# Pool's convolution taps in accumulators of their own, and two TensorE steps moved, in a two-layer hybrid decoder trunk

## The chip, the cores and the metric

The kernel runs on one core of one Trainium2 chip. A core has five engines that run side by side, each with its own queue of instructions: TensorE (PE, matmuls; PEld is its weight load), VectorE (DVE), ScalarE (ACT), GpSimd (POOL) and SyncE (SP, which issues DMAs; POOL issues some too). An engine takes its instructions in the order in which they were written, so one that waits holds up all behind it. The metric is the device time of one execution in microseconds; smaller is better.

## The reference

Two layers (`DEPTH = 2`) of width 1024 over 256 positions. Each layer is a SwiGLU FFN, a token-mixing stage and a second FFN, each with adaLN modulation. The change lies in the mixing stage, which projects its normalised input once and works on three groups of columns:

```
h = a * sigmoid(gate)                                   # group A, 256 channels
h = depthwise_causal_conv(h, w)  # 31 taps; then LayerNorm over channels, SiLU

softmax attention, 6 heads of 64 with partial rotary    # group B

q, k, v = silu(short_conv(qkv))                         # group C, 6 heads of 64, chunked delta rule
g = cumsum(-exp(a_log) * softplus(a + dt_bias));  beta = sigmoid(b)
L = strict_lower(k_beta k^T * decay(g));  T = inverse(I + L)
u = T v_beta, ...;  o = rmsnorm(...) * silu(z)
```

The three outputs are concatenated and go through one output projection. All arithmetic is float32; matmuls split their operands into a high and a low part and use three products.

## The kernel before, in words

All weights (253 MB in the profile) are streamed through four raw buffers of 1 MB by SP's queue. ACT rounds each piece to a high part (`hi`), DVE subtracts for the low part (`lo`), and PE multiplies. The adaLN vectors are summed by DVE from their own weight pieces (`adaacc`, `Lb`).

The instruction order is fixed when the program is written, by a planner inside the kernel. `Clock` keeps a modelled time for each engine and for each tile the modelled time at which it is ready. The main stream of PE is the projection, unit by unit; after each step of it, `tick()` goes through a list of side generators (`sides`): key and query norms, decays, pairs, gate and convolution, values, inverse, delta rule, attention, taps. A generator that yields tiles, such as `yield (v,)`, goes on once these are ready by the modelled clock; `yield from until("v")` waits for an event of that name, and `room()` for a free PSUM bank. What a generator then emits stands in the engines' queues at that place, whatever the real times are.

The parts that the change touches:

- `decays()` computes the log decays' exponentials. `spread(b)` has DVE write 128x1024 spread rows into `Rs` (tiles `Lb` and `S6a`); a small product of `g[:, 0]` (tile `g_g`) with the constant `gt` gives `cross` (tile `g_c`), the bias of one of the three exponentials of each head. Before the change this product stands directly behind the emission of the first two spreads.
- `values_beta()` turns v (tile `v`) by six PE transposes into `vb`, as soon as `gate_conv()` has emitted v's SiLU (event `v`). `delta_rule()` is the first to use `vb`, after the event `inverse`.
- `inverse()` inverts I + L. The matrix LT (tile `xin_LT`, views `LD` and `LX`) is written to memory (`scr_l`, by `pairs()`) and read back as `Lb`, both by POOL's DMA queue; POOL then does a substitution of 15 steps on 16x16 blocks (tiles `T` and `W`), writes the result to `scr_w` and reads it back as `Wc`; PE, ACT and DVE join the blocks. While the substitution is planned, `cfg["lo_pool"]` is False, and taps go to DVE alone.
- `tap(b, fast)` does one of the 31 taps of channel block b (b = 0, 1) on the 128x256 accumulator `cacc["ca"][:, b]` (tile `cacc`). The first is a DVE `tensor_scalar`; a fast one is a DVE `scalar_tensor_tensor`; a slow one has ACT write the product into a tile `ctap` (two buffers) and POOL add it to the same accumulator. `taps(b)` takes the slow form where DVE is over 2 us ahead of PE by the modelled clock; `fill()` puts a tap where DVE would stand still.
- `convolution()` sums the accumulators over the channels, normalises and applies SiLU; the output projection of blocks 0 and 1 follows.

The tags `rstd` and `gr` name two small buffers (the norm's reciprocal roots, the gates' rows) whose contents have been used up when the taps begin.

Nearly all engine calls go through one helper, so nearly every row of the profile says L171, and instructions are told apart by their tiles (`pa`, `pm` and `px` are PSUM banks).

Of the kernel before, what the change touches and what calls it, by code (L numbers as in the profile page):

```python
# [10 lines left out]
F32 = mybir.dt.float32  # L11
# [3 lines left out]
OP = mybir.AluOpType  # L15
# [4 lines left out]
S = 256  # L20
# [5 lines left out]
NH = 6  # L26
# [151 lines left out]
def trunk(ctx, tc, t, out):  # L178
# [5 lines left out]
    act, dve, pe, gp, sp, qd = (clock.engine(n, e) for n, e in (  # L184
        ("act", nc.scalar), ("dve", nc.vector), ("pe", nc.tensor), ("gp", nc.gpsimd), ("dma", nc.sync), ("dma2", nc.gpsimd)))

    def sb(shape, tag, dt=F32, bufs=1):
        return clock.tile(tag, bufs, pool.tile(shape, dt, name=tag, tag=tag, bufs=bufs))
# [10 lines left out]
    def mm(o, lhsT, rhs, start, stop=True):  # L199
        pe.matmul(o, lhsT, rhs, start=start, stop=stop, skip_group_check=True)  # L200
# [55 lines left out]
    p = ps([128, 128], "x")  # L256
# [753 lines left out]
    def mixing(l, G, normed, nxt):  # L1010
# [4 lines left out]
        ev = {}  # L1015
# [21 lines left out]
        def room(n=1):  # L1037

            while True:
                times = sorted(freed(x) for x in side_tags() if x not in held.values())  # L1040
                if len(times) > n and times[n - 1] <= clock.t["pe"]:
                    return
                yield

        def pside(shape, hold=False):
            tag = min((x for x in side_tags() if x not in held.values()), key=freed)
            p = latest[tag] = ps(shape, tag)
            if hold:
                held[p.tensor.name] = tag
            return p  # L1050
# [7 lines left out]
        def until(*names):  # L1058
            while any(n not in ev for n in names):
                yield  # L1060
# [137 lines left out]
        def decays():  # L1198
            yield from until("g", "kconv")
            g, lnbeta = ev["g"], ev["lnbeta"]  # L1200
            while any(job[1].tensor.name.startswith("Lb") for job in ada_wait):
                extract()
            g, heads = g
            Rs = [sb([128, 1024], tag, F32R).rearrange("p (s k i x) -> p s k i x", s=2, k=2, i=2) for tag in ("Lb", "S6a")]
            cross = sb([128, NH], "g_c")

            def spread(b):
                dve.tensor_tensor(Rs[b % 2].rearrange("p s k i x -> p (s k i) x"), K["tri"][:, 0:128].unsqueeze(1).to_broadcast([128, 8, 128]),
                                  heads[:, 2 * b:2 * b + 2].rearrange("p h k i -> p (h k i)").unsqueeze(2).to_broadcast([128, 8, 128]),
                                  op=OP.mult)  # L1210

            spread(0)
            spread(1)
            yield from room()
            p = pside([128, NH])
            mm(p, gt.bitcast(F32), g[:, 0], True)
            dve.tensor_tensor(cross, p, lnbeta[:, 0, NH:], op=OP.add)
            for b in range(3):
                R = Rs[b % 2]
                yield (R,)  # L1220
                yield from room(2)
                d = pside([128, 2, 2, 128], True)
                x = pside([128, 2, 128], True)
                for k in range(2):
                    mm(d, gt, R[:, :, k], k == 0, False)
                mm(d, identb, negdb.unsqueeze(1).to_broadcast([128, 4, 128]), False, True)
                for k in range(2):
                    mm(x, onesr, R[:, :, k, 1], k == 0, k == 1)
                if b == 0:
                    spread(2)  # L1230
                yield from until("ktable")
                yield (x,)
                let_go(d)
                let_go(x)
                for s in range(2):
                    h = 2 * b + s
                    act.activation(PT[:, h, 0:128], d[:, s, 0], AF.Exp, bias=lnbeta[:, 0, NH + h:NH + h + 1])
                    act.activation(PT[:, h, 128:256], x[:, s], AF.Exp, bias=cross[:, h:h + 1])
                    act.activation(PT[:, h, 256:384], d[:, s, 1], AF.Exp, bias=lnbeta[:, 1, NH + h:NH + h + 1])
                    ev["decay", h] = True  # L1240
            yield from until("kh")
            act.preload_act_table_set("silu_and_others")
            ev["silu2"] = True
# [31 lines left out]
            ev["PT"] = True  # L1275

        def values_beta():
            yield from until("v")
            v = ev["v"]
            vb = sb([128, 2, 384], "vb")  # L1280
            for i in range(2):
                yield (v,)
                yield from room()
                p = pside([128, 384])
                for b in range(3):
                    pe.transpose(p[:, 128 * b:128 * b + 128], v[:, b, HALF[i]], ident)
                act.copy(vb[:, i], p)
            ev["vb"] = vb
# [81 lines left out]
        def inverse():  # L1370
# [21 lines left out]
                yield idle("gp")  # L1392
            gp.tensor_copy(W[:, 1], V.rearrange("p c i -> p i c"))
            cfg["lo_pool"] = True
            C = sb([128, 2, 12, 32], "Wc")
            for f in range(2):
                for i in range(2):
# [17 lines left out]
            p, o = joined()  # L1415
# [8 lines left out]
            p, o = joined()  # L1424
# [17 lines left out]
            p, o = joined()  # L1442
# [53 lines left out]
            ev["exp2"] = True  # L1496


        cacc, left = {}, {}

        def tap(b, fast=True):

            hc, ca, k = ev["glu"], cacc["ca"], left[b] - 1
            wof = CB["conv_w"]
            w = cB[:, wof + 2 * k + b:wof + 2 * k + b + 1]
            if k == CONVK - 1:
                dve.tensor_scalar(ca[:, b], hc[:, b, k:k + S], w, cA[:, CA["conv_b"] + b:CA["conv_b"] + b + 1],
                                  op0=OP.mult, op1=OP.add)
            elif fast:
                dve.scalar_tensor_tensor(ca[:, b], hc[:, b, k:k + S], w, ca[:, b], op0=OP.mult, op1=OP.add)  # L1510
            else:
                m = sb([128, S], "ctap", bufs=2)
                act.activation(m, hc[:, b, k:k + S], AF.Copy, scale=w)
                gp.tensor_tensor(ca[:, b], ca[:, b], m, op=OP.add)
            left[b] = k

        def fill():
# [7 lines left out]
        def taps(b):  # L1525
            yield from until("glu")
            if "ca" not in cacc:
                cacc["ca"] = sb([128, 2, S], "cacc")
            left[b] = CONVK
            clock.filler = fill  # L1530
            while left[b]:
                yield idle_any(("dve",), ("act", "gp")) if cfg["lo_pool"] else idle("dve")
                if left[b]:
                    tap(b, left[b] == CONVK or clock.t["dve"] <= clock.t["pe"] + AHEAD)
            ev["taps", b] = True

        def convolution():
            yield from until(("taps", 0), ("taps", 1), "exp2")
            ca = cacc["ca"]
            yield (ca,)  # L1540
            yield from room()
            p = pside([128, S], True)
            for b in range(2):
                mm(p, ones, ca[:, b], b == 0, b == 1)
            yield soon(p)
            let_go(p)
            dve.scalar_tensor_tensor(ca, p.unsqueeze(1).to_broadcast([128, 2, S]), -1.0 / 256, ca, op0=OP.mult, op1=OP.add)
            sq = tmp([128, 2, S])
            yield (ca,)
            act.activation(sq, ca, AF.Square)  # L1550
            yield (sq,)
            yield from room()
            p = pside([128, S], True)
            for b in range(2):
                mm(p, ones, sq[:, b], b == 0, b == 1)
            r = tmp([128, S])
            yield soon(p)
            let_go(p)
            act.activation(r, p, AF.Ln, bias=eps, scale=1.0 / 256)
            act.activation(r, r, AF.Exp, scale=-0.5)  # L1560
            yield (r,)
            dve.tensor_tensor(ca, ca, r.unsqueeze(1).to_broadcast([128, 2, S]), op=OP.mult)
            yield from until("softmaxed", "zraw", *["gdn_normed"] * ("u" in ev))
            act.preload_act_table_set("silu_and_others")
            act.activation(ev["zraw"], ev["zraw"], AF.Silu)
            ev["z"] = ev["zraw"]
            for b in range(2):
                act.activation(ca[:, b], ca[:, b], AF.Silu, scale=cA[:, CA["conv_ln_g"] + b:CA["conv_ln_g"] + b + 1],
                               bias=cA[:, CA["conv_ln_b"] + b:CA["conv_ln_b"] + b + 1])
            act.copy(yh[:, 0:2], ca)  # L1570
            dve.tensor_tensor(yl[:, 0:2], ca, yh[:, 0:2], op=OP.subtract)
            ev["conv_done"] = True
# [420 lines left out]
```

## Time and profile before

| | us |
|---|---|
| median of three runs | 1190.27 |
| lowest and highest | 1187.80, 1190.31 |
| the profiled execution, its own time | 1185.86 |
| span of the profiled execution, first to last instruction | 1184.1 |
| PE busy | 1118.8 (94%) |
| DVE busy | 880.2 (74%) |
| ACT busy | 596.9 (50%) |
| POOL busy | 142.0 (12%) |

The mean granted TensorE clock is 0.980 of full speed. A busy PE is not PE at its peak. In the span the first layer's mixing stage lies roughly between 250 and 400 us, the second's between 820 and 975; the rest is FFNs. A row of the timeline has the start, the duration, the engine, the operation and its tiles, the count, and in brackets the idle time of the engine just before it with what ended it. A row of the table of stretches gives each engine's busy time in that stretch, then the granted clock.

### The profile page before, as it was taken

How to read it: one execution, taken by the hardware profiler on the slowest of the kernel's cores; microseconds unless marked ns; L12 is line 12 of the kernel's file. 1: busy time of each engine (PE TensorE's matmuls, PEld its weight loads, DVE VectorE, ACT ScalarE, POOL GpSimd, SP SyncE). 2: the span in 40 equal slices, each digit the busy share in tenths (PEclk: the TensorE clock that was granted, in tenths of full speed). 3: DMA queues.
4: the chain of work that ended last, by engine and by line, in shares of the span. 5: the costliest groups of instructions: out<-in, count | busy, mean ns of one | idle time of the engine just before them, and what ended most of it. 6: DMA issues, size and time to landing. Idle time of an engine off the chain costs nothing. (4 is left out here: it accounts for less than half of the span.)

```text
span 1184.1 us, 21996 instructions
## 1 busy us (share of the span) xinstructions
PE 1118.8 (94%) x9085; PEld 1042.9 (88%) x9085; DVE 880.2 (74%) x1354; ACT 596.9 (50%) x1007; POOL 142.0 (12%) x185
## 2 busy tenths in 40 slices
PE   5799999999899689999999999999989998999997
PEld 4799999967778689999999999997768898999996
DVE  6778778757897788868779878773869959766554
ACT  4364444447366364544456544434743676544443
POOL 0710000010650010000001000001037101000002
PEclk9899999999999989999999999999998999999999
DMA  9759888836333558968864997793552325876740
GB/s 325 249 174 353 291 309 311 245 105 201 99 127 123 174 182 290 328 236 320 302 227 161 329 333 256 279 302 92 168 165 74 144 81 170 304 247 214 203 136 36
DMA packets 167660, 256.52 MB, mean 217 GB/s; under 512 B 8272, under 2 KB 134056, under 8 KB 167560
## 3 DMA queue, kind: packets, MB, share of 16 engines
q1 hardware_dynamic: 166536, 252.95, 63.1%
q0 software_dynamic: 1024, 2.16, 0.9%
q8 instruction: 71, 1.16, 0.4%
q14 instruction: 29, 0.24, 0.1%
HBM read 252.86 MB, written 2.23 MB: 215 GB/s over the span
## 5 line engine op out<-in xcount | busy, mean ns | idle before, releaser
L171 PE MATMUL pm<-H,hi 128*128 128x256 f32 x2816 | 509.2, 283 | 1.2 <-DVE H L171 1.2
L171 DVE TENSOR_TENSOR lo<-raw,hi 128x1024 fp32r<-128x1024 f32 (+1 forms) x300 | 362.6, 1230 | 101.2 <-ACT hi L171 100.3
L171 PEld LDWEIGHTS pm<-H,hi 128*128 128x128 f32 x2816 | 432.3, 189 | 5.1 <-issue 1.6
L171 ACT CAST hi<-raw 128x1024 fp32r<-128x1024 f32 (+1 forms) x306 | 311.4, 1041 | 190.7 <-PE pm L171 77.0
L171 PE MATMUL pm<-H,lo 128*128 128x256 f32 x1408 | 392.1, 280 | 0.0
L171 PEld LDWEIGHTS pm<-H,lo 128*128 128x128 f32 x1408 | 264.8, 189 | 0.0
L171 PE MATMUL pa<-Y,hi 128*128 128x256 f32 x1312 | 235.3, 283 | 3.5 <-DVE xT L171 2.7
L171 PEld LDWEIGHTS pa<-Y,hi 128*128 128x128 f32 x1312 | 201.6, 190 | 4.7 <-DVE xT L171 3.5
L171 PE MATMUL pa<-Y,lo 128*128 128x256 f32 x656 | 184.1, 281 | 0.0
L171 PEld LDWEIGHTS pa<-Y,lo 128*128 128x128 f32 x656 | 125.8, 192 | 0.0
L171 POOL TENSOR_TENSOR xin_LT<-xin_LT 128x256 f32<-128x256 f32 x35 | 27.2, 776 | 667.5 <-ACT xin_LT L171 665.1
L171 ACT CAST Y<-tmp 128x256 fp32r<-128x256 f32 x88 | 35.8, 406 | 121.2 <-DVE tmp L171 121.2
L171 DVE SCALAR_TENSOR_TENSOR adaacc<-raw,c_act,adaacc 128x1024 f32<-128x1024 f32 x70 | 94.2, 1346 | 1.6
L171 DVE SCALAR_TENSOR_TENSOR Lb<-raw,c_act,Lb 128x1024 f32<-128x1024 f32 x56 | 71.8, 1282 | 4.3 <-DMA raw<-in_w_ada_dram 3.0
L171 DVE TENSOR_TENSOR Y<-tmp,Y 128x256 fp32r<-128x256 f32 x88 | 37.4, 425 | 41.6 <-ACT Y L171 41.6
L171 PE MATMUL pm<-Y,raw 128*128 128x256 f32 x288 | 67.5, 384 | 0.0
L171 PEld LDWEIGHTS pm<-Y,raw 128*128 128x128 f32 x288 | 53.1, 190 | 7.9
L171 PE MATMUL pa<-hi,Y 128*128 128x512 f32 x176 | 54.8, 393 | 0.0
L171 DVE SCALAR_TENSOR_TENSOR cacc<-hc,colB,cacc 128x256 f32<-128x256 f32 x94 | 47.9, 528 | 8.0 <-POOL cacc L171 6.8
L171 ACT ACTIVATE tmp<-pm 128x256 f32<-128x256 f32 x78 | 29.6, 380 | 47.7 <-PE pm L171 47.7
L171 DVE TENSOR_REDUCE mod<-px 128x4 f32<-128x512 f32 x34 | 23.4, 690 | 38.4 <-PE px L171 38.4
L171 POOL TENSOR_TENSOR cacc<-cacc,ctap 128x256 f32<-128x256 f32 x26 | 26.0, 1010 | 131.0 <-ACT ctap L171 126.0
(303 smaller groups left out, 1311.2 us busy)
## 6 DMA issues: line engine op xcount, KB each, us to landing
raw<-in_w_ada_dram SPq DMA_DIRECT2D x70, 1024.0 KB
raw<-in_ffn_w_gate_dram SPq DMA_DIRECT2D x44, 1024.0 KB
raw<-in_ffn_w_up_dram SPq DMA_DIRECT2D x44, 1024.0 KB
raw<-in_ffn_w_down_dram SPq DMA_DIRECT2D x44, 1024.0 KB
raw<-in_w_in_dram SPq DMA_DIRECT2D x12, 1024.0 KB
raw<-in_w_in_dram SPq DMA_DIRECT2D x20, 512.0 KB
raw<-in_w_out_dram SPq DMA_DIRECT2D x16, 512.0 KB
raw<-in_w_in_dram SPq DMA_DIRECT2D x4, 768.0 KB
```

Source lines behind the costliest of these rows:

```text
L171: return getattr(real, op)(*args, **kw)
```

## The change

Three edits in `mixing()`.

1. Pool's taps get accumulators of their own, one for each channel block, in the buffers `rstd` and `gr`. The first slow tap of a block is written there by ACT without a POOL instruction; each later one is a product of ACT in `ctap` and an addition of POOL to that accumulator. `convolution()` begins with a DVE addition of each such accumulator to `ca`.
2. `values_beta()` also waits for a new event `back`, which `inverse()` sets when the substitution has been emitted.
3. In `decays()` the product for `cross` moves behind the wait for the first spread rows.

```
@@ decays @@
             spread(0)
             spread(1)
-            yield from room()
-            p = pside([128, NH])
-            mm(p, gt.bitcast(F32), g[:, 0], True)
-            dve.tensor_tensor(cross, p, lnbeta[:, 0, NH:], op=OP.add)
             for b in range(3):
                 R = Rs[b % 2]
                 yield (R,)
+                if b == 0:
+                    yield from room()
+                    p = pside([128, NH])
+                    mm(p, gt.bitcast(F32), g[:, 0], True)
+                    dve.tensor_tensor(cross, p, lnbeta[:, 0, NH:], op=OP.add)
                 yield from room(2)
@@ values_beta @@
-            yield from until("v")
+            yield from until("v", "back")
@@ inverse @@
             gp.tensor_copy(W[:, 1], V.rearrange("p c i -> p i c"))
             cfg["lo_pool"] = True
+            ev["back"] = True
@@ tap @@
-        cacc, left = {}, {}
+        cacc, left, shared = {}, {}, set()
...
+            other = cacc["gp"][b]
...
             else:
-                m = sb([128, S], "ctap", bufs=2)
+                m = sb([128, S], "ctap", bufs=2) if b in shared else other
                 act.activation(m, hc[:, b, k:k + S], AF.Copy, scale=w)
-                gp.tensor_tensor(ca[:, b], ca[:, b], m, op=OP.add)
+                if b in shared:
+                    gp.tensor_tensor(other, other, m, op=OP.add)
+                shared.add(b)
@@ taps @@
                 cacc["ca"] = sb([128, 2, S], "cacc")
+                cacc["gp"] = [sb([128, S], tag) for tag in ("rstd", "gr")]
@@ convolution @@
             ca = cacc["ca"]
+            for b in sorted(shared):
+                yield (cacc["gp"][b],)
+                dve.tensor_tensor(ca[:, b], ca[:, b], cacc["gp"][b], op=OP.add)
             yield (ca,)
```

## The prediction

> **What bounds the kernel now.** I read the page's busy shares first, then who PE (TensorE) waited for, over the whole run.
>
> ```profile
> span 1184.1 us, 21996 instructions
> ...
> PE 1118.8 (94%) x9085; PEld 1042.9 (88%) x9085; DVE 880.2 (74%) x1354; ACT 596.9 (50%) x1007; POOL 142.0 (12%) x185
> ```
>
> ```profile
> PE pa L171 <- ACT v L171: 9.2, 2, 4.7
> ...
> PE pa L171 <- DVE g_g L171: 3.2, 2, 1.6
> ```
>
> PE is the bound, so time is gained only where PE stands still or runs slowly. Columns of the waits: total, times, longest. Both lines occur twice, once in each layer's mixing stage, and the diff's second and third edits move exactly these two PE instructions. The timeline of the first layer shows how the longer wait comes about (start, duration, instruction; in brackets the engine's idle time before it, and its releaser).
>
> ```profile
> 290.58 0.61 DVE L171 TENSOR_TENSOR xin_LT<-pa,PT 128x256 f32<-128x256 f32 x2
> ...
> 295.85 0.73 POOL L171 TENSOR_TENSOR cacc<-cacc,ctap 128x256 f32<-128x256 f32 x1 [52.44 <-ACT ctap L171]
> 296.52 2.48 POOL L171 DMA_DIRECT2D scr_l<-xin_LT  x4
> 296.88 0.51 ACT L171 ACTIVATE ctap<-hc,colB 128x256 f32<-128x256 f32 x1
> ...
> 304.03 1.45 POOL L171 DMA_DIRECT2D Lb<-scr_l  x2 [5.03 <-DMA scr_l<-xin_LT]
> 305.50 0.75 POOL L171 TENSOR_TENSOR cacc<-cacc,ctap 128x256 f32<-128x256 f32 x1
> 306.28 0.88 DVE L171 SCALAR_TENSOR_TENSOR cacc<-hc,colB,cacc 128x256 f32<-128x256 f32 x2 [2.69 <-POOL cacc L171]
> 307.07 1.51 DVE L171 SCALAR_TENSOR_TENSOR v<-pm,colB,v 128x255 f32<-128x255 f32 x3
> 308.66 1.28 ACT L171 ACT_TABLE_LOAD   x1 [6.47 <-DVE v L171]
> ...
> 310.85 0.90 PE L171 MATMUL pa<-kc,v 128*128 128x128 f32 x3 [4.50 <-ACT v L171]
> ```
>
> The product of Pool's second tap was ready at 297.4 (296.88 plus 0.51), but its addition stands in POOL's queue behind the DMA that reads `scr_l` back, and that one waits for the write to land. DVE's next tap on the same accumulator therefore waits 2.69, v's convolution behind it on DVE is late, ACT's table load and SiLU of v are late, and PE stands at the transposes of v, with all matmuls behind them.
>
> A second thing stands there: the matrix LT (`xin_LT`) was complete at 291.2, yet POOL issued its DMA at 296.5, because the first tap's addition was ahead in the queue, waiting for ACT. The second layer repeats all of it:
>
> ```profile
> 864.69 0.61 DVE L171 TENSOR_TENSOR xin_LT<-pa,PT 128x256 f32<-128x256 f32 x2
> ...
> 870.63 2.45 POOL L171 DMA_DIRECT2D scr_l<-xin_LT  x4
> ...
> 880.56 0.88 DVE L171 SCALAR_TENSOR_TENSOR cacc<-hc,colB,cacc 128x256 f32<-128x256 f32 x2 [2.86 <-POOL cacc L171]
> ...
> 885.14 0.90 PE L171 MATMUL pa<-kc,v 128*128 128x128 f32 x3 [4.67 <-ACT v L171]
> ```
>
> After each of these waits the granted clock (the column behind POOL's) is low; this is the table of stretches:
>
> ```profile
> core 0: us, PE busy (x) PEld busy (x) DVE busy (x) ACT busy (x) POOL busy (x), PEclk, DMA share, GB/s
> 310.85:313.50 2.65, 2.65 (x7) 1.51 (x8) 1.07 (x4) 2.51 (x5) 2.18 (x7) 0.50 0.00 0
> 885.14:890.40 5.26, 5.26 (x19) 4.12 (x20) 3.66 (x8) 4.19 (x7) 4.40 (x12) 0.50 0.01 3
> 904.30:911.10 6.80, 6.80 (x28) 6.17 (x29) 6.66 (x16) 3.04 (x9) 6.52 (x8) 0.50 0.25 58
> ```
>
> **The change, part by part.**
>
> *Values behind the substitution.* The six transposes of v are emitted only after Pool's substitution has been planned, so later in PE's stream, when v is long done. They and ACT's two copies into `vb` stay as many as before. `vb` is first used by the delta rule, after the inverse, so nobody is behind them. PE loses the wait: 4.50 + 4.67 = 9.2. It also loses the half clock behind it: 2.65 and 5.26 us at 0.50 cost half, 1.3 + 2.6 = 3.9. What is late next on PE are the query products, which need the same SiLU and the table load behind it; the order is planned again, and they stay where the planned time of the queries puts them, so other matmuls fill the gap. That the third stretch (904.3 to 911.1, no wait before it) goes too, worth 3.4, I don't count; it is the fast end.
>
> [...]
>
> *Pool's own accumulators.* The first slow tap of each of the two channel blocks becomes one ACT instruction that writes the accumulator directly; its POOL addition goes. The other additions stay, on Pool's own tile. DVE's chain no longer waits for POOL: 2.69 and 2.86 less DVE waiting, so v's SiLU is that much earlier (in the gain above already, since PE no longer waits for v). Nothing of POOL is ahead of the `scr_l` DMA any more, so it can issue at 291.2 instead of 296.5: 5.3 earlier in each layer. Added: one DVE addition per block at the end, 128x256, two a layer, each below the 0.68 of DVE's 128x512 product in the next fence. Their cover:
>
> ```profile
> 377.18 0.68 DVE L171 TENSOR_TENSOR cacc<-cacc,tmp 128x512 f32<-128x512 f32 x1
> ...
> 386.28 1.28 ACT L171 ACT_TABLE_LOAD   x1
> ```
>
> The normalised convolution is done at 377.9 and used only after the table load that waits for PE's z, at 386.3: 8.4 us hide at most 1.4. If PE reaches z 7 us earlier than now and the taps don't follow, 1.4 is left, just enough. If the cover were gone it would cost up to 1.4 a layer.
>
> *Log decays' product behind the spread rows.* The product needs g, the end of a DVE chain of small operations; PE meets it too early:
>
> ```profile
> 259.65 0.17 DVE L171 TENSOR_TENSOR g_g<-g_x,g_ea 128x12 f32<-128x12 f32 x1
> ...
> 259.88 0.39 PE L171 MATMUL pa<-g_g,gt 128*128 128x6 f32 x2 [1.61 <-DVE g_g L171]
> ...
> 267.50 0.63 ACT L171 ACTIVATE tmp<-S3a 128x512 f32<-128x512 f32 x1
> ...
> 268.19 1.12 PE L171 MATMUL pa<-tmp,kc 128*128 128x512 f32 x2
> ```
>
> ```profile
> 834.00 0.39 PE L171 MATMUL pa<-g_g,gt 128*128 128x6 f32 x2 [1.62 <-DVE g_g L171]
> ```
>
> The waits are 1.61 and 1.62, together 3.2, and go. The bounds of what stays are 0 and 3.2: the key norm's product at 268.19 starts 0.06 after its squares are ready (267.50 plus 0.63), which DVE and ACT set, so PE can lose there what it gained, unless the new order puts more matmuls ahead. The order does count PE's wait for g in its plan, so some will move; between the ends I take half, 1.6. DVE's small addition behind the product comes later in DVE's queue, and ACT's exponentials need it; a delay there is within that half.
>
> *What takes the place.* The next thing that PE can meet is the first product of the inverse, which needs Pool's whole chain (LT to `scr_l`, back, substitution, `scr_w`, back as `Wc`):
>
> ```profile
> 330.06 2.09 POOL L171 DMA_DIRECT2D Wc<-scr_w  x2
> ...
> 334.38 1.01 PE L171 MATMUL pa<-Wc,Lb 32*32 32x32 f32 x96
> ```
>
> ```profile
> 903.87 2.09 POOL L171 DMA_DIRECT2D Wc<-scr_w  x2
> ...
> 912.77 1.02 PE L171 MATMUL pa<-Wc,Lb 32*32 32x32 f32 x96
> ```
>
> ```profile
> DMA to landing us min/median/max: 4.0/4.1/4.3
> ```
>
> ```profile
> 291.20:334.40 43.20, 38.66 (x233) 32.86 (x233) 33.36 (x72) 18.38 (x34) 29.20 (x53) 0.96 0.41 119
> 865.30:912.90 47.60, 42.93 (x245) 36.85 (x247) 37.91 (x79) 22.43 (x46) 31.96 (x55) 0.86 0.39 108
> ```
>
> `Wc` lands 4.1 after its issue, at 334.2 and 908.0: the chain takes 43.0 and 42.7 from LT. 5.3 earlier makes 37.7 and 37.4. PE's own work in the same stretches, at full clock, is 38.66 less 1.3 = 37.3 and 42.93 less 6.0 (half of 5.26 + 6.80) = 36.9. So new waits of 0.4 and 0.5 come out. The unknown is when `scr_l` lands: issued earlier, it runs beside other weight transfers. Bounds: 0 (the chain fully hidden) and 11.4 (nothing of the 5.3 gained: 5.7 + 5.8). I take 2.0, near the worked value.
>
> **The sum.** 9.2 + 3.9 + 3.2 gained is 16.3; 1.6 and 2.0 come back; 12.7 stay. The profiled execution took 1185.9 (span 1184.1), so 1173.2 for it. The median of the three runs shown is 1190.3, 4.4 above it; taken from the median the forecast is 1177.6. The tails of both layers and the FFNs behind hang on PE's progress and shift with it.
>
> **The rivals.**
>
> *A: Pool's chain becomes the wait.* `scr_l` lands no earlier, since the transfers beside it hold it up (POOL waited 5.03 for it even now). Then the first layer's stretch stays at 43.0 of 43.2 and the second's comes to 42.7 of 47.5: gains 0.2 and 4.8, plus 1.6 from the log decays: 6.6, time 1183.7. For it: the window is just as full of weights. Against it: the write starts 5.3 earlier in any case. Chance 0.15.
>
> *B: everything goes.* Nothing comes back and the half clock at 904 goes too: 16.3 + 3.4, time 1170.6. Chance 0.11.
>
> *C: no change.* A, with the log decays' 3.2 lost whole at the key norm and the half clock at 904 coming again (3.4), leaves 1.6: 1188.7. Chance 0.07.
>
> *D: slower, DVE and POOL block each other.*
>
> ```profile
> L171 DVE SCALAR_TENSOR_TENSOR cacc<-hc,colB,cacc x94: 465/484/1224, 296.0 to 944.3; 128x256 f32<-128x256 f32 x94
> L171 POOL TENSOR_TENSOR cacc<-cacc,ctap x26: 722/742/1712, 295.8 to 928.8; 128x256 f32<-128x256 f32 x26
> ```
>
> ```profile
> L171 POOL TENSOR_TENSOR cacc<-cacc,ctap 128x256 f32<-128x256 f32 x26 | 26.0, 1010 | 131.0 <-ACT ctap L171 126.0
> ```
>
> ```profile
> 295.00:386.00 91.00, 83.67 (x916) 71.06 (x916) 74.42 (x161) 49.84 (x110) 38.47 (x61) 0.96 0.37 118
> ```
>
> POOL's addition takes 0.72 alone and up to 1.71 beside DVE; DVE's tap 0.48 and up to 1.22. On one accumulator they took turns; on two they run at once, and with POOL free of the chain the plan may give it more taps, 20 a layer instead of 13. If each blocks DVE for 0.99, DVE has 20 x 0.99 = 19.8 more, less today's excess (13 additions a layer at a mean of 1.01 instead of 0.72: 3.8) and 7 taps that it no longer does (3.4): 12.6, with the two final additions 13.4. That makes 87.8 of the 91.0. The layer gets longer from the point where over 3.2 of today's 16.6 us of DVE idle can't be filled; with half of them, 96.1, 5.1 more a layer, less the log decays' 3.2: 1197.3. Against it: the plan gives POOL a tap only when DVE is ahead. Chance 0.07.
>
> [...]
>
> **How the numbers follow.** The forecast (gain 9 to 16, 1174 to 1181) has 0.60, with A 0.15, B 0.11, C 0.07, D 0.07. About 0.2% (2.4 us) is what a measurement of this kernel can tell from no change. Faster: 0.60 + 0.15 + 0.11 = 0.86; same 0.07; slower 0.07. The range takes in B and A, with 3 us above A for part of C: 1170 to 1187.
>
> **What the profile after would show.** Right: PE's list of waits has no `v` and no `g_g`; `scr_l` is issued within 1 us of LT's last DVE product; DVE never waits for POOL's `cacc`; the granted clock stays at 1.00 where the transposes of v were; two DVE additions a layer with Pool's tiles. Wrong: PE waits over 2 us before the first `pa<-Wc,Lb` product (A), before `pa<-tmp,kc` at the key norm, or before the query products; or POOL's additions are many and near 1.7 us (D). What would upset the forecast most is the planned order itself: it is computed anew from the first moved instruction on, and a matmul placed before its operand stops PE as v did.

## The result, and the profile after

The changed kernel takes 1201.62 us (median; 1197.41 to 1206.52) beside 1190.29 for the kernel before: a ratio of 1.0107 [1.008, 1.0133] (in brackets, here and below, the 95% interval). The forecast was 1177.6, faster. The profiled execution took 1198.98, its span is 1197.2, 13.1 longer than before's.

The busy shares, and who PE waited for, in the changed kernel:

```profile
span 1197.2 us, 22024 instructions
...
PE 1129.8 (94%) x9085; PEld 1052.4 (88%) x9085; DVE 880.5 (74%) x1351; ACT 601.4 (50%) x1015; POOL 155.3 (13%) x195
```

```profile
PE pa L171 <- DMA Wc<-scr_w: 13.0, 2, 7.6
PE pa L171 <- ACT Y L171: 7.3, 3, 5.2
...
PE pa L171 <- DVE E L171: 3.5, 1, 3.5
```

The columns are total, times, longest. The waits for `v` (9.2) and `g_g` (3.2) are gone, as forecast. A wait for `Wc` of 13.0 stands in their place. And PE executes the same 9085 matmuls but is busy 11.0 us longer: they ran at a lower clock (0.965 in the mean, 0.980 before). The table of stretches shows where. Each layer's mixing stage is cut in two: its *front*, from the first product of the projections (`pm<-S6a,wab`) to the first product of `Wc`, and its *end*, from there to the next `px<-kc,adaacc`. First the kernel before (front, end, front, end), then the changed one:

```profile
237.20:334.40 97.20, 91.00 (x458) 70.34 (x459) 68.79 (x159) 48.88 (x102) 34.71 (x62) 0.98 0.45 132
334.40:401.70 67.30, 60.24 (x804) 52.79 (x804) 50.91 (x102) 43.13 (x94) 9.27 (x9) 0.97 0.33 116
811.30:912.80 101.50, 95.17 (x459) 74.23 (x460) 71.92 (x162) 51.86 (x112) 34.86 (x59) 0.93 0.41 118
912.80:977.50 64.70, 64.09 (x847) 56.53 (x847) 48.60 (x97) 43.27 (x87) 7.35 (x6) 1.00 0.36 123
```

```profile
237.00:345.70 108.70, 102.63 (x548) 82.49 (x548) 80.75 (x176) 61.46 (x129) 41.52 (x66) 0.99 0.50 154
345.70:402.30 56.60, 48.15 (x653) 40.22 (x653) 35.27 (x68) 29.06 (x61) 8.44 (x10) 0.75 0.22 68
815.00:926.20 111.20, 103.48 (x548) 83.00 (x548) 78.58 (x168) 62.57 (x130) 46.01 (x65) 0.99 0.51 155
926.20:990.20 64.00, 61.14 (x753) 51.47 (x754) 40.95 (x91) 32.16 (x68) 3.47 (x4) 0.81 0.17 51
```

Length less PE busy is PE's idle time; length times (1 less the granted clock) is what half clock took. In the ends the clock fell from 0.97 and 1.00 to 0.75 and 0.81: half clock took 67.3 x 0.03 = 2.0 there before, and takes 56.6 x 0.25 + 64.0 x 0.19 = 26.3 now. In the fronts it fell, from 97.2 x 0.02 + 101.5 x 0.07 = 9.0 to 2.2. The fronts became 11.5 and 9.7 longer and hold 90 and 89 matmuls more; the ends became 10.7 and 0.7 shorter. Both stages together are 9.8 longer; 3.1 more lie between the two (412.7 instead of 409.6), where the 61 matmuls that left the first layer's stage (458 + 804 before, 548 + 653 now) are made up for.

The timeline shows what made `Wc` late. DVE's queue in the kernel before, and in the changed kernel:

```profile
268.14 1.22 DVE L171 TENSOR_TENSOR S6a<-kc,g_r 128x1024 fp32r<-128x1024 f32 x1
269.27 0.16 DVE L171 TENSOR_TENSOR g_c<-pa,g_x 128x6 f32<-128x6 f32 x1
```

```profile
269.11 0.75 DVE L171 TENSOR_SCALAR adaacc<-raw,c_act 128x1024 f32<-128x1024 f32 x1
269.89 1.28 DVE L171 SCALAR_TENSOR_TENSOR adaacc<-raw,c_act,adaacc 128x1024 f32<-128x1024 f32 x1
271.09 2.42 DVE L171 SCALAR_TENSOR_TENSOR Q<-pm,colB,Q 128x255 f32<-128x255 f32 x6
273.43 2.35 DVE L171 TENSOR_TENSOR lo<-raw,hi 128x1024 fp32r<-128x1024 f32 x2
275.70 0.69 DVE L171 TENSOR_TENSOR S3a<-S3a,tmp 128x512 f32<-128x512 f32 x1
276.30 0.16 DVE L171 TENSOR_TENSOR g_c<-pa,g_x 128x6 f32<-128x6 f32 x1
```

Then ACT's exponentials, the last products of LT (four in 1.14, so LT is complete at 300.05 instead of 291.2), POOL's queue, and PE:

```profile
276.55 0.37 ACT L171 ACTIVATE PT<-pa,g_c 128x128 f32<-128x128 f32 x1 [2.31 <-DVE g_c L171]
...
298.91 1.14 DVE L171 TENSOR_TENSOR xin_LT<-pa,PT 128x256 f32<-128x256 f32 x4
...
296.89 2.33 POOL L171 TENSOR_TENSOR rstd<-rstd,ctap 128x256 f32<-128x256 f32 x3 [53.76 <-ACT ctap L171]
301.34 3.32 POOL L171 TENSOR_TENSOR rstd<-rstd,ctap 128x256 f32<-128x256 f32 x4 [2.12 <-ACT ctap L171]
304.62 0.93 POOL L171 TENSOR_TENSOR gr<-gr,ctap 128x256 f32<-128x256 f32 x1
305.48 2.48 POOL L171 DMA_DIRECT2D scr_l<-xin_LT  x4
...
339.93 2.09 POOL L171 DMA_DIRECT2D Wc<-scr_w  x2 [0.35 <-issue]
...
345.72 1.50 PE L171 MATMUL pa<-Wc,Lb 32*32 32x32 f32 x96 [5.34 <-DMA Wc<-scr_w]
```

In this first layer `g_c` is 7.0 later, LT 8.9. By then the convolution's input is there, so eight of Pool's additions stand in POOL's queue ahead of the DMA of `scr_l`; it is issued 5.4 after LT is complete. The second layer does the same (eight additions, `scr_l` at 882.83, 4.3 after LT, `Wc` at 920.29, PE's wait 7.63).

### The profile page after: what moved, and what is told of

It is laid out like the page before. It is cut to its first block, busy times and chain, and to the rows that moved or that the text cites. A ratio compares the mean times of both kernels' runs of the same rounds, so it can differ in the third digit from the quotient of the medians.

```text
span 1197.2 us, 22024 instructions
## 1 busy us (share of the span) xinstructions
PE 1129.8 (94%) x9085; PEld 1052.4 (88%) x9085; DVE 880.5 (74%) x1351; ACT 601.4 (50%) x1015; POOL 155.3 (13%) x195
## 4 chain that ended last, share of the span: by engine, by line
PE 76%; DVE 8%; POOL 6%; DMA 4%; ACT 3%; issue 2%; SPq 0%; POOLq 0%; DVEq 0%; ACTq 0%
PE pm L171 45%; PE pa L171 29%; DVE adaacc L171 2%; PE px L171 2%; DVE lo L171 2%; POOL W L171 2%; DMA raw<-in_w_in_dram 1%; POOL T L171 1%; POOL xin_LT L171 1%; DMA Wc<-scr_w 1%; ACT hi L171 1%; POOL Lb L171 1%; DVE S3a L171 1%; DVE mod L171 1%; DMA xin_LT<-in_x_dram 1%
## 5 line engine op out<-in xcount | busy, mean ns | idle before, releaser
L171 PE MATMUL pa<-Y,hi 128*128 128x256 f32 x1312 | 241.2, 286 | 9.8 <-ACT Y L171 7.3
L171 DVE SCALAR_TENSOR_TENSOR cacc<-hc,colB,cacc 128x256 f32<-128x256 f32 x80 | 41.9, 543 | 1.2
L171 DVE TENSOR_TENSOR tmp<-tmp,pm 128x256 f32<-128x256 f32 x80 | 33.2, 415 | 11.4 <-ACT tmp L171 11.4
```

Source lines behind the costliest of these rows:

```text
L171: return getattr(real, op)(*args, **kw)
```

## The experiments

Each ratio is to the kernel before on the same chip. *Part 1* is Pool's accumulators (the hunks in `tap`, `taps`, `convolution`), *part 2* the values (`"back"`), *part 3* the log decays' product.

**The parts apart and in pairs.** Each of these is the diff with some hunks left out.

Part 3 alone:

> Only the log decays' product is moved; values and Pool's taps as before. Theory T (the moved product makes DVE's addition g_c late, so LT is late and Pool's taps get ahead of the scr_l DMA): g_c at about 276 instead of 269.3, LT about 300 instead of 291, 6 additions ahead of scr_l in POOL's queue, scr_l issued 5 us or more later, PE waits 5 us or more for Wc in each layer; slower than before, 1196 to 1206. Rival A1 (Pool's new accumulators are what hurts, the moved product is worth its 3.2 us): 1186 to 1190. Rival D (DVE and POOL block each other on two accumulators, which this kernel doesn't have): also 1186 to 1190.

1.0022 [1.0004, 1.0039]: `g_c` at 277.15, LT at 300.90, six additions ahead of `scr_l`, which goes out at 306.21, all as T says. But PE waits for `Wc` in the second layer alone (9.6; in the first it reaches that product without a wait), and the loss is 0.2% instead of 1%: at 1191.6 the time lies between the ranges of T and of its rivals.

Parts 1 and 2:

> The changed kernel with the log decays' product back in front of the spread rows; Pool's accumulators and the later values stay. T: g_c at 269.3, LT at 291, no addition ahead of scr_l, scr_l issued within 1 us of LT, no PE wait for v, PE waits for Wc at most 2 us a layer; the log decays' waits of 1.6 are back. Forecast's sum without its log decays: 9.2 + 3.9 less 2.0, so 1176 to 1182. A1 and D: as slow as the changed kernel or 3 us slower, 1198 to 1206.

0.9985 [0.9963, 1.0006]. LT and `scr_l` come as T says (`scr_l` at 291.44). But the gain is 0.15%, not clear of no change, instead of 1%; T isn't the whole. These are the first front and end and the second front, and PE's waits for the first product of `Wc`:

```profile
237.30:331.10 93.80, 89.51 (x458) 69.52 (x458) 69.22 (x162) 48.30 (x101) 32.88 (x59) 1.00 0.46 137
331.10:403.60 72.50, 63.75 (x804) 55.96 (x804) 52.24 (x98) 44.09 (x97) 11.59 (x15) 0.91 0.31 108
815.30:909.10 93.80, 89.43 (x455) 69.42 (x454) 68.01 (x159) 47.40 (x99) 30.53 (x55) 1.00 0.44 128
```

```profile
331.08 1.01 PE L171 MATMUL pa<-Wc,Lb 32*32 32x32 f32 x96 [2.62 <-DVE Y L171]
...
909.13 1.01 PE L171 MATMUL pa<-Wc,Lb 32*32 32x32 f32 x96 [2.72 <-DMA Wc<-scr_w]
```

The fronts are 3.4 and 7.7 shorter than before's: together 11.1, which is the forecast's 9.2 + 3.9 - 2.0 to the tenth. That is luck, since the terms differ: PE's idle time in the fronts fell by 3.9, where 9.2 - 2.0 = 7.2 was forecast, and its busy time by 7.2, where the half clock's 3.9 was forecast (the stretch at 904, left out of the forecast, went too). Both ends give the gain back: 72.5 and 70.1, 5.2 and 5.4 more. In the first end half clock takes 72.5 x 0.09 = 6.5 (2.0 before), idle time 8.8 (7.1); in the second half clock takes 4.9 (none before).

Parts 2 and 3:

> The changed kernel with Pool's taps back on the common accumulator; later values and the moved product stay. T: LT still late, 6 additions ahead of scr_l, PE waits 5 us or more for Wc a layer: 1196 to 1206, the changed kernel within 0.4%. A1 and D: the loss was Pool's accumulators, so 1176 to 1184.

1.0106 [1.0062, 1.015]: as slow as the changed kernel. A1 falls: Pool's accumulators are not needed for the loss. But here too PE waits for `Wc` in the second layer alone (8.6), not in each layer as T says.

Parts 1 and 3:

> Pool's accumulators and the moved log decays' product; the values stay in front. Alone, part 1 gave 0.28% and part 3 cost 0.22%; parts 2 and 3 together cost 1.06%. If the loss is an interaction of the later values with the late LT (no dense work left for the stage's end): this pair is near the sum of its parts, 1185 to 1191. If part 3 with any companion loses (LT late, Pool's taps ahead of scr_l): 1195 to 1204.

1.0071 [1.0044, 1.0099]. So the later values aren't needed either: part 3 costs 0.2% alone, and 0.9 to 1.2% beside part 1, part 2 or both.

Part 1 alone, and part 2 alone:

> Only Pool's accumulators of its own; values and log decays' product as before. Before's v waits (9.2 us) come from DVE standing behind Pool's second tap; with that tie cut v is ready earlier, so if part 1 does what it was forecast to do by itself, PE's wait for v falls to under 4 us in sum, and the time is 1180 to 1186. If the pair of parts 1 and 2 gained nothing because the chain to Wc and what follows it sets the end of the stage (waits only move), this one too is within 0.4% of before: 1184 to 1192.

> Only the values behind the substitution; Pool's taps on the common accumulator and the log decays' product as before. Forecast's mechanism: 9.2 of waits and 3.9 of half clock go, 1176 to 1182, with PE waiting for Wc a little more than in the pair. If waits only move: 1184 to 1192, with new PE waits of 6 us or more in sum before the products of Wc, Y or E in the same stage.

Part 1: 0.9972 [0.9952, 0.9992], PE's wait for `v` down from 9.2 to 3.3. Part 2: 1.0019 [0.9999, 1.0039], no gain though the wait for `v` is gone. The query products stand in its place, not those of `Wc`, `Y` or `E` as expected, each wait as long as two thirds of the old one:

```profile
PE pa L171 <- DVE Q L171: 6.0, 2, 3.2
```

**Pool's taps kept behind the substitution.** The planner may give POOL a tap only from the event that part 2 sets:

```
-                yield idle_any(("dve",), ("act", "gp")) if cfg["lo_pool"] else idle("dve")
+                yield idle_any(("dve",), ("act", "gp")) if "back" in ev else idle("dve")
```

> The changed kernel, but Pool gets no tap before the substitution has been planned; LT is as late as in the changed kernel. Tells apart what the late LT does by itself from what the additions ahead of scr_l add. If the additions carry the loss: scr_l issued at about 300.3 instead of 305.5, substitution back to 13 to 14.5 us, PE's wait for Wc 0 to 3 us a layer, 1182 to 1191. If the late LT alone carries it: the wait for Wc stays above 4 us, 1195 to 1203.

0.9932 [0.9911, 0.9953]; at 1179.52 that is 2.5 below the range given for the additions. In a second series of the same kernel:

> The changed kernel with the bar on Pool's taps, as run before (ratio 0.9932), for more times on the chip and an ordinary trace: 1176 to 1183, granted clock 0.979, half clock in the two stages' ends below 12 us in sum where the changed kernel lost 25.

0.9956 [0.9935, 0.9977]; 1184.70 is 1.7 above the range expected. One edit turns 1.1% lost into 0.4 to 0.7% gained, with `g_c` and LT as late as in the changed kernel (276.56 and 299.67). `scr_l` goes out as LT is complete, and PE has no wait for `Wc` in either layer (rows of the second series):

```profile
299.76 2.48 POOL L171 DMA_DIRECT2D scr_l<-xin_LT  x4 [56.26 <-DVE xin_LT L171]
...
333.91 2.09 POOL L171 DMA_DIRECT2D Wc<-scr_w  x2
```

```profile
344.50:394.00 49.50, 45.08 (x684) 38.50 (x683) 42.42 (x81) 28.75 (x63) 12.73 (x12) 0.93 0.38 129
...
914.20:968.50 54.30, 49.16 (x708) 43.51 (x708) 44.00 (x80) 36.65 (x75) 13.20 (x14) 0.87 0.40 135
```

The last two rows are the ends. Half clock takes 3.5 and 7.1 there, where the changed kernel lost 14.2 and 12.2.

The bar with the product in front as before (parts 1 and 2), and with parts 1 and 3:

> Parts 1 and 2, the log decays' product in front as before, and Pool gets no tap before the substitution has been planned: like the run with taps after, but with LT at 291 instead of 300. If keeping taps off POOL, DVE and ACT until then is what gains by itself: 1176 to 1183. If that run's gain needed the moved product (3.2 us of waits for g, 1.6 each, gone with it): 1182 to 1188, the g waits back in the list.

> Parts 1 and 3 with the bar on Pool's taps, the values in front as before. If the gain of the bar doesn't need the later values (which alone cost 0.19%): 1176 to 1182, at or below the bar kernel. If it needs them: 1184 to 1192.

0.9963 [0.9949, 0.9977] and 0.9947 [0.9921, 0.9972]. The times, 1184.12 and 1183.08, do not decide by the ranges: the first lies in the range for a gain that needs the moved product, the second between its two. But the second series of the bar is no faster, and the four series with it are not clearly apart. Beside part 3 the bar is what turns a loss into a gain, with the later values (1.0107 to 0.9956) or without (1.0071 to 0.9947). With the product in front, where no addition is ahead of `scr_l` anyway, what it adds is not clear (0.9985 to 0.9963), and part 1 alone gains 0.28% without it.

**Is it POOL's queue, or the work of the taps elsewhere?**

```
-                if b in shared:
+                if b in shared and "back" in ev:
                     gp.tensor_tensor(other, other, m, op=OP.add)
+                elif b in shared:
+                    clock.note("gp", "tensor_tensor", (other, other, m), {})
```

> The changed kernel with Pool's additions ahead of the substitution left out (their ACT products still run; these taps are missing from the convolution's sum). Every other instruction of all engines stands in the changed kernel's order. scr_l then issues when LT is ready, at about 300 instead of 305.5 in the first layer. If the additions in POOL's queue carry the loss: Wc issued at 334 to 336, PE's waits for Wc (13.0 us) gone but for 3 us at most, 1182 to 1192. If the other order on PE, ACT and DVE carries it: 1194 to 1201.

0.9994 [0.9973, 1.0016], 1187.07 beside 1188.58 for the kernel before: the whole loss is gone with nothing taken away but POOL's additions planned ahead of the substitution.

```profile
300.38 2.48 POOL L171 DMA_DIRECT2D scr_l<-xin_LT  x4 [56.95 <-DVE xin_LT L171]
...
335.69 2.09 POOL L171 DMA_DIRECT2D Wc<-scr_w  x2
...
341.65 1.01 PE L171 MATMUL pa<-Wc,Lb 32*32 32x32 f32 x96 [1.04 <-DMA Wc<-scr_w]
```

In the first layer `Wc` is issued 4.2 earlier than in the changed kernel, and PE's wait for it falls from 13.0 to 1.0 over both. ACT's and DVE's taps and PE's order, all kept, do not carry the loss. A rival is that the additions slow DVE's instructions beside them; DVE is busy 878.4 instead of 880.5 over the run, with the same 1351 instructions, so this is no more than 2.1 of the 13 us that are won back. Half clock still takes 18.5 in the ends (clock 0.81 and 0.87): that alone does not make the kernel slower than before's.

The other way round, such additions put into the kernel before, and into part 1 alone:

```
...
             yield (LD,)
+            for _ in range(12):
+                nc.gpsimd.tensor_tensor(late_by, LD[:, 5], LD[:, 5], op=OP.add)
```

> The kernel before with 12 useless additions (128x256, both inputs the last LT block, 0.72 to 0.75 us each, 9 us in sum) on POOL between LT and the scr_l DMA; every other instruction of all engines stands in before's order. scr_l at about 305 instead of 296.5, as in the changed kernel. If a Wc that comes 9 us late is enough for the loss: PE waits 7 to 9 us for Wc in each layer and the time is 1200 to 1210. If what hides it is large (PE's other waits shrink by as much): 1190 to 1196.

1.0091 [1.0059, 1.0123]. The time, 1199.80, is 0.2 below the range, and the reason is another: PE does not wait for `Wc`, it waits for `v`:

```profile
PE pa L171 <- ACT v L171: 20.2, 2, 10.1
```

Before's second tap stands behind the read of `scr_l`, as the prediction described (in the second layer the read is issued at 893.62, the tap's addition starts at 895.08), and holds DVE's taps and `v`. Part 1 cuts this tie, so the same 12 additions (9.08 together in the second layer here) were put between LT and the DMA of `scr_l` in part 1 alone, which takes 1183.78 without them:

> [...] If a late Wc is enough by itself: no wait for v beyond the 3.3 that are there, PE waits 6 to 9 us for Wc in each layer, and the time is 1194 to 1206. If the loss needs the tie or the other order of the changed kernel: 1184 to 1190.

1.0109 [1.0082, 1.0136], 1.4% (16 us) over part 1 alone (0.9972), for `scr_l` issued 8.8 after LT in each layer (292.22 and 301.04). PE's waits now:

```profile
PE pa L171 <- DMA Wc<-scr_w: 8.1, 2, 4.7
PE pa L171 <- ACT v L171: 7.9, 2, 4.0
```

So additions that make `scr_l` 8.8 late cost about that length in each layer, with no other change of order. Less of it than expected shows as a wait for `Wc` (4.7 and 3.4); the wait for `v` grew from 3.3 to 7.9, and DVE was busy 886.8 instead of 881.7 beside the added additions, 5.1 of the 16 that the late `scr_l` may not account for.

**What takes the clock in the ends?** In the trace of before, 128 dense matmuls of the side work on `H` (128*128 in their rows, 48 of them 128x384) stand behind `Wc`'s first product in the first end and lie between the inverse's small ones. In the changed kernel 44 are left, none of them wide: PE used the rest up in the longer front. Useless dense products were put in to tell whether the half clock goes with PE's standing still or with thin work. First in front of `Wc`'s first product, unseen by the planner:

```
...
+            for _ in range(20):
+                mm(p[:, 0:128], K["blk"], K["tri"][:, 0:128], True)
...
             for m in range(12):
                 for q in QUAD:
                     mm(o[q, m], Um[q, m], C[q, 1, m], True)
```

> The changed kernel with 20 useless 128x128 products on PE in front of the first product of Wc in each layer, where PE waits 5.3 and 7.6 us; the order of everything else is the changed kernel's. Their work is some 3.5 to 5 us a layer at full clock, less than the wait, so by themselves they cost nothing. If the half clock after these waits (345.7 to 357 in the first layer, 926 to 930 in the second, 7.6 us lost) comes from PE standing still: 1190 to 1196, clock 0.970 or more. If it comes from the stage's thin work (few matmuls at a time, waits on DVE and ACT): no change, 1198 to 1204. If the products delay the chain: slower.

1.0093 [1.0066, 1.012]. PE's waits for `Wc` fell from 13.0 to 5.7 (1.9 and 3.9) and the time did not: clock 0.73 and 0.82 in the ends, as in the changed kernel. Then six such products in front of each of seven later groups of the inverse:

> The changed kernel with 6 useless 128x128 products on PE in front of seven of the inverse's later groups of products in each layer: about 1.3 us of dense work at full clock each, 9 us a layer, none in front of the first product of Wc; the order of everything else is the changed kernel's. If the half clock of the stage's end comes from too little dense work there: granted clock 0.974 or more (the changed kernel had 0.965), loss of half clock down by 8 us or more, and the time at or below the changed kernel's in spite of 18 us of added work: 1188 to 1202. If half clock has another cause: clock 0.966 or less, time 1204 to 1222.

1.0165 [1.0145, 1.0184]; the granted clock of the run is 0.974, as expected of thin work, but the time missed the range by 7 us.

```profile
345.40:409.00 63.60, 56.41 (x737) 48.91 (x737) 34.56 (x68) 29.19 (x61) 8.47 (x10) 0.83 0.19 60
935.40:1000.20 64.80, 62.74 (x836) 55.45 (x837) 40.91 (x91) 32.19 (x68) 4.09 (x5) 0.96 0.16 50
```

In the second layer 11 us of useless work at full clock (busy time less half clock is 62.74 - 2.6 instead of 61.14 - 12.2) made the end only 0.8 longer, since half clock took 2.6 instead of 12.2. In the first layer it took 10.8 instead of 14.2, and the end grew by 7.0. So in the second end the clock goes with how thin the work there is (0.96 with the dense products, 0.81 without), more than with the wait for `Wc` ahead of it (0.82 with the products placed there); in the first end (0.83 instead of 0.75) the products brought back only a quarter of the loss, and what takes the rest there is not shown.

**The product as soon as g is planned.** Part 3 in another place, in front of the spread rows' products, then the same with the bar:

```
             spread(1)
+            yield (g[:, 0],)
             yield from room()
             p = pside([128, NH])
```

> The changed kernel, but the log decays' product stands where g is planned to be ready, in front of the spread rows' products: DVE's addition g_c then stands behind two adaacc operations only, at about 271.4 instead of 276.3 (269.3 before). If DVE's late addition is the step that failed: PE's wait for g gone, LT at 292 to 294, dense work back behind Wc, 1178 to 1188. If the order of the taps and the values is what fails, whatever LT does: 1195 to 1204.

1.0168 [1.0145, 1.0191], the slowest of all and above both ranges (1209.81). `g_c` at 272.07 and LT at 294.98 are within 1 us of what was hoped. But two of Pool's additions (3.84) still stand ahead of `scr_l`, which goes out at 299.00, 4.0 after LT, and POOL does 42 additions over both layers (36 in the changed kernel). PE stands 5.2 in front of the first product of `Wc` in each layer:

```profile
PE pa L171 <- POOL rstd L171: 10.4, 2, 5.2
```

The profile puts these waits down to an addition of POOL that ended just then; `Wc` had been issued 4.3 before the product started, as far ahead as in the first layer of part 1 alone with the 12 additions, where PE waits for `Wc` (335.33, 339.63), so its landing may be the true cause. With the bar:

> The same, and Pool gets no tap before the substitution has been planned. With LT at 292 to 294 and nothing of Pool's taps ahead of scr_l: the run with taps after and the product in front (1184.1), less the 3.2 us of waits for g: 1178 to 1184. If the taps no longer matter once LT is early: the same as the run without this bar.

1.0007 [0.9997, 1.0017], 1190.05 where 1178 to 1184 was expected: the miss that tells most. `scr_l` goes out at 293.88, 0.1 after LT. The fronts and ends:

```profile
237.40:331.80 94.40, 94.40 (x489) 74.59 (x487) 69.53 (x167) 52.80 (x113) 33.41 (x59) 1.00 0.50 146
331.80:402.70 70.90, 63.82 (x772) 54.92 (x771) 51.23 (x92) 40.83 (x87) 17.23 (x15) 0.86 0.31 107
812.10:906.50 94.40, 94.40 (x492) 74.60 (x494) 68.31 (x164) 51.64 (x109) 31.00 (x54) 1.00 0.48 137
906.50:983.80 77.30, 69.48 (x814) 60.90 (x814) 55.16 (x95) 45.25 (x92) 17.24 (x15) 0.85 0.34 113
```

PE runs through both fronts without a gap and at full clock: all the waits that the change aims at are gone, none has taken their place there, and the fronts are 2.8 and 7.1 shorter than before's. The ends are 3.6 and 12.6 longer, with 9.9 and 11.6 of half clock.

## Why the prediction was wrong

- *The waits for v and g go.* Right: neither is in the list, and DVE no longer waits for POOL's `cacc`.
- *"DVE's small addition [`g_c`] behind the product comes later in DVE's queue ...; a delay there is within that half."* This step failed first. The term was 1.6 for both layers. In the first layer the addition came 7.0 later, behind 7 us of DVE's own queue, and LT 8.9 later. The prediction priced PE's place of the product and not the queue of the engine that takes it over.
- *"Nothing of POOL is ahead of the scr_l DMA any more, so it can issue at 291.2."* This step failed at the greatest cost: it holds for the first tap of each block, and only while LT comes before the taps, as in parts 1 and 2 alone (291.44). With LT late, eight additions were ahead, and `scr_l` went out at 305.48. "What takes the place" was taken as 2.0 out of bounds of 0 to 11.4; the wait for `Wc` measured 13.0. Leaving the additions out undoes the whole loss. (In the second layer the working of this term also took out the half clock at 904, which the sum does not count.)
- *The half clock behind the waits goes (3.9).* The two stretches behind `v` did. But the whole run's clock fell (0.980 to 0.965), because half clock moved into the ends (2.0 to 26.3). There it goes, as the run with dense products in the ends shows for the second layer (clock 0.96 with them, 0.81 without), with how much dense work is left, and the prediction had no term for that.
- *"The tails of both layers and the FFNs behind hang on PE's progress and shift with it."* Failed, and it is why even parts 1 and 2, whose fronts gained 11.1, show no gain that is clear of no change (0.15%). The ends took it back. Which of the operations on DVE and ACT sets their length stays open: the runs show only that PE idles there and runs slowly.
- *The rivals.* A had the place right (`Wc` becomes the wait) and the sign wrong: it took `scr_l` to be issued earlier in any case. D ended on the right side by another mechanism: the changed kernel's DVE taps at a median of 0.484 are no slower than before, and POOL's additions number 36 instead of 26, not 40. D's place, POOL's taps, was right. B came true in the fronts of the last run alone, and its ends took it back. The prediction did name the order that is planned anew as its largest risk, but looked for it in a matmul ahead of its operand; it came as additions ahead of a DMA.
- *Open:* why part 3 alone lost only 0.2% with six additions ahead of `scr_l`. PE's waits for `Wc` do not tell (9.6 there, 8.6 in parts 2 and 3, which lost 1.06%). Half clock in the ends goes with the loss better: 14 us in part 3 alone, 26 to 30 in the changed kernel, parts 2 and 3, and parts 1 and 3. No run isolates this.

## What to carry to other kernels

Before a producer is moved to a later place, look at the queue of the engine that consumes it and at the queues behind that, up to the next DMA: a 0.16 us operation set 8.9 us of a chain here. Keep optional work out of a queue that also issues the DMAs of a critical chain; here a bar of one line turned a loss of 1.1% into a gain of 0.4 to 0.7%. A wait removed ahead of a stretch of small products can bring nothing, since that stretch can get longer by as much (fronts 11.1 shorter and ends 10.6 longer in parts 1 and 2, 9.9 and 16.2 in the last run), so add up idle time and half clock over both.

## What the hardware showed that was not expected

PE ran at half clock for 18 us while its records show it busy all the time, in the changed kernel's second end:

```profile
938.00:956.00 18.00, 18.00 (x190) 13.21 (x189) 13.40 (x37) 8.24 (x24) 1.68 (x3) 0.50 0.05 15
```

In the same stretch after `Wc`'s first product, the kernel with useless dense products there shows 251 matmuls at full clock:

```profile
947.00:965.00 18.00, 18.00 (x251) 14.90 (x250) 14.07 (x39) 8.50 (x25) 1.93 (x3) 1.00 0.09 32
```

Both stretches show PE busy throughout. Whether the size of the matmuls (152 of the 190 in the first use 32 or 64 rows) or gaps that the records hide make the difference, no run here shows.

Pool's substitution got slower; its two instructions, before and after:

```profile
L171 POOL TENSOR_TENSOR W<-W,T 96x15 f32<-96x15 f32 (+7 forms) x30 | 11.7, 390 | 2.3
L171 POOL TENSOR_TENSOR T<-W,Lb 96x15 f32<-96x15 f32 (+7 forms) x30 | 11.0, 367 | 5.2 <-DMA Lb<-scr_l 3.0
```

```profile
L171 POOL TENSOR_TENSOR W<-W,T 96x15 f32<-96x15 f32 (+7 forms) x30 | 15.9, 529 | 2.4
L171 POOL TENSOR_TENSOR T<-W,Lb 96x15 f32<-96x15 f32 (+7 forms) x30 | 13.9, 464 | 4.4 <-DMA Lb<-scr_l 2.2
```

That is 7.1 us more over both layers, on the chain to `Wc`. With the additions ahead of it left out, the two take 25.9 instead of 29.8, and with the bar (second series) 26.9, still more than the 22.7 of before. No run isolates where the rest comes from.
